# Four output blocks begun together, the first norm moved under the next products, and longer distances between the steps of the head work

## The chip, the cores and the metric

The kernel runs on one core of a Trainium2 chip. The metric is the device time of one execution in microseconds (us). Engines are named as in the profile: PE is TensorE (PEld its weight loads), DVE is VectorE, ACT is ScalarE, POOL is GpSimd, SP is SyncE, which issues nearly all the transfers.

## The reference

One layer of a streaming encoder is computed for two groups of rows that share all weights: 256 prompt rows and 64 rows that continue an earlier stream. Model width is 2048, so the activations are 320 columns wide when they are held feature by feature (16 blocks of 128 features).

```python
h = rmsnorm(x, g_pre_mix);  p = h @ w_in                     # 2048 -> 6144 + 16
a = conformer_conv(value, gate)      # GLU, causal depthwise conv of width 31, group norm, silu
q, k, v = silu(short_conv_4(qkv));  q, k = l2norm(q), l2norm(k)
beta = sigmoid(b);  g = -exp(a_log) * softplus(a_raw + dt_bias)
o, state = gated_delta_chunked(q, k, v, g, beta, state)
b = rmsnorm_per_head(o) * silu(z)
x = x + rmsnorm(concat(a, b) @ w_out, g_post_mix)
h = rmsnorm(x, g_pre_ffn)
gate, up = split(causal_dwconv_3(h @ w_up))                  # 2048 -> 2 * 5632
x = x + rmsnorm((silu(gate) * up) @ w_down, g_post_ffn)
```

The chunked delta rule needs, per chunk and head, the inverse of a unit lower triangular matrix. Outputs are the new rows and the new states of the convolutions and of the delta rule. All values are float32.

## The kernel before, in words

**Products.** Every large product is taken in float32 accuracy by splitting both operands into a rounded part and a rest: `hi` (a copy into the matmul format, ACT, line 174) and `lo` (the difference, DVE, line 175). A block of 128 output columns over half of the depth (8 of 16 feature blocks) takes 24 matmuls of 128x320: 8 times hi*hi (line 190) and hi*lo (line 191), then 8 times lo*hi (line 194). This text calls these matmuls "products" and such a set of 24 a half block. A weight half block is one transfer of 512 KB into one of three buffers `w`; its split goes into one of three pairs `whi`, `wlo`.

**The norm of the input.** The split of x uses x times the gain and not the normed x; the factor per row, `rb`, is multiplied in when a finished block is read from PSUM. So products can start before the norm is known, and everything that reads a finished block waits for `rb`. `rb` comes from sums of squares: a matmul with ones (`pst`, line 212), a small DVE operation and a power on POOL (`rr`, lines 215 and 216), a matmul that spreads it over the partitions (`psb`, line 222), and a copy on ACT.

**The opening.** x and the weights of two blocks (the gate and value of the first convolution block, `first`) are loaded in five groups of k-blocks, 2, 2, 4, 4 and 4 of them. For each group ACT makes hh (line 291) and whi, DVE makes hl and wlo. Squares of x are taken by ACT for two quarters (line 302) and by POOL for two (line 304), and added by DVE (lines 319 and 320). Then come 32 matmuls for the gates (`psba`, lines 249 and 250) on weights `wbz` that are loaded after all those of the opening.

**The plan.** A string orders the blocks of the input projection: `c` is a convolution block (gate and value products, then DVE's 30 taps on `cvt`, line 441), `g` the gates, `h` a head (three blocks, q, k and v, read by DVE and POOL into `qb`, short convolution `cq` at line 504), `z` a head's output gate. Then come 15 blocks of the output projection over 12 of the 16 depth blocks (`psm`), its rest (`psm2`), and the feed-forward part.

**Jobs.** What follows a block (the tail of a convolution block, of a head, the inverse and the recurrence of a pair of heads, the gates) is a generator that yields distances, counted in products: `tick` counts each product, and every 20th it advances the jobs that are due. A job's instructions stand behind the product counted last; within that, the tile scheduler orders each engine's instructions by priority. `finish` empties a job at once, whatever its distances: the tail of convolution block i-2 before block i goes on to its own tail, and pair i-2 before head 2i begins. The order on each engine is fixed when the kernel is built.

The steps that matter here: `pt_c` (line 450) transposes a finished convolution block, its statistics go over DVE, POOL and ACT (`un`), and a second set of transposes (line 465, in the profile also under the name pt_c) brings it back, LAG_STAT later. Head tails make the matrix `np` (line 584) from `pk`, `pks` and the decay factors `E`, which POOL multiplies (line 408) from `psd` (line 404) and `rg` (line 401). A pair's inverse writes `np` to DRAM, reads diagonal blocks back (`dn`), solves them on DVE, and brings the result back through DRAM as `wtp`; LAG_BASE later its first matmuls `pz` (line 652) read `wtp`. After the recurrence, LAG_NORM lies ahead of the transposes `pt_o` (line 781).

PSUM has eight banks: two for blocks (`ps_p`), two for transposes (`ps_t`), four for jobs (`ps_g`).

## Time and profile before

| what | before |
|---|---|
| median of 3 runs (lowest, highest) | 1569.41 us (1567.59, 1575.73) |
| profiled execution, its span | 1568.74 us, 1566.9 us |
| PE, DVE, ACT, POOL busy, share of the span | 97%, 64%, 47%, 21% |
| granted clock, mean | 0.985 |
| input projection and head work | from the opening to about 482.6 us |
| feed-forward part | from about 640 us |

A PE that is busy 97% of the span is read with care: the table of stages shows that its idle time lies nearly all in the first 500 us, and that the granted clock is below full there. So the time is read by where PE waits, by what ended each wait, and by the stretches of half clock behind the waits.

### The profile page before, as it was taken

The page shows a single profiled execution, that of the slowest core. Times are in us where ns is not written, and L with a number is a line of the kernel's source. Part 1 is how long each engine was busy: PE and PEld are TensorE (multiplying, and loading weights), DVE is VectorE, ACT ScalarE, POOL GpSimd, SP SyncE. Part 2 cuts the span into 40 slices and gives each one's busy share as a digit, 9 for nine tenths or more (in the row PEclk, how much of TensorE's full clock was granted, in tenths as well). Part 3 has the DMA queues.
Part 4 walks back from the last instruction along what each step waited for, and adds up shares of the span by engine and source line. Part 5 has one row for each costly group of instructions (what it writes and reads, how often), then busy time and mean ns, then how long its engine had stood idle before and what let it go on. Part 6 is the DMA issues. An engine that isn't in the chain of part 4 may idle for free.

```text
span 1566.9 us, 26507 instructions
## 1 busy us (share of the span) xinstructions
PE 1521.0 (97%) x10247; PEld 1496.3 (95%) x10249; DVE 1009.1 (64%) x1824; ACT 732.2 (47%) x1199; POOL 333.0 (21%) x503
## 2 busy tenths in 40 slices
PE   7998999999989999999999999999999999999998
PEld 6988989999989998899999999999999999999997
DVE  6778869786788567866534665644666544666554
ACT  5664454554635465544434444433444433444453
POOL 4352222242221000122200232200222200222101
PEclk9999999999999999999999999999999999999999
DMA  7435335353443573344455545455444455554453
GB/s 236 141 99 146 107 111 155 111 161 96 117 124 106 152 243 115 117 148 148 123 154 168 150 148 156 126 152 172 149 149 148 133 149 172 150 152 148 134 148 113
DMA packets 95767, 224.31 MB, mean 143 GB/s; under 512 B 18328, under 2 KB 37016, under 8 KB 95512
## 3 DMA queue, kind: packets, MB, share of 16 engines
q1 hardware_dynamic: 95640, 222.61, 47.2%
q8 instruction: 81, 1.33, 0.3%
q14 instruction: 46, 0.38, 0.1%
HBM read 215.45 MB, written 7.12 MB: 142 GB/s over the span
## 4 chain that ended last, share of the span: by engine, by line
PE 80%; DVE 9%; POOL 3%; DMA 3%; ACT 2%; issue 2%; SPq 0%; DVEq 0%; ACTq 0%; POOLq 0%
PE psu L190 12%; PE psu L191 12%; PE psu L194 12%; PE psdn L190 7%; PE psdn L191 7%; PE psdn L194 7%; DVE wlo L175 3%; PE psq L194 2%; PE psq L190 2%; PE psq L191 2%; DVE cvt L441 2%; PE psm L194 2%; PE psm L191 2%; PE psm L190 2%; DMA wtp<-wsp 1%
## 5 line engine op out<-in xcount | busy, mean ns | idle before, releaser
L174 ACT CAST whi<-w 128x1024 fp32r<-128x1024 f32 (+3 forms) x441 | 421.6, 957 | 553.0 <-PE psu L191 172.7
L175 DVE TENSOR_TENSOR wlo<-w,whi 128x1024 fp32r<-128x1024 f32 (+3 forms) x441 | 487.4, 1105 | 186.6 <-ACT whi L174 103.5
L190 PE MATMUL psu<-hi,whi 128*128 128x320 f32 x1344 | 398.2, 310 | 2.9 <-DVE fbuf L980 2.9
L191 PE MATMUL psu<-lo,whi 128*128 128x320 f32 x1344 | 397.9, 310 | 0.0
L190 PEld LDWEIGHTS psu<-hi,whi 128*128 128x128 f32 x1344 | 253.2, 188 | 3.4 <-DVE fbuf L980 3.4
L191 PEld LDWEIGHTS psu<-lo,whi 128*128 128x128 f32 x1344 | 253.1, 188 | 0.0
L981 POOL COPY nffn<-fbuf 128x2 f32<-128x2 f32 x88 | 100.5, 1142 | 597.9 <-DVE fbuf L979 597.2
L194 PE MATMUL psu<-hi,wlo 128*128 128x320 f32 x1344 | 224.8, 309 | 0.0
L191 PE MATMUL psdn<-gl,whi 128*128 128x320 f32 x704 | 208.9, 310 | 0.0
L190 PE MATMUL psdn<-gh,whi 128*128 128x320 f32 x704 | 208.7, 310 | 0.0
L194 PEld LDWEIGHTS psu<-hi,wlo 128*128 128x128 f32 x1344 | 203.9, 188 | 0.0
L979 DVE TENSOR_TENSOR fbuf<-psu,rb 128x256 f32<-128x256 f32 x88 | 37.4, 425 | 176.9 <-PE psu L194 174.4
L441 DVE SCALAR_TENSOR_TENSOR cvt<-ub,par,cvt 128x350 f32<-128x350 f32 x240 | 137.5, 589 | 2.6
L190 PEld LDWEIGHTS psdn<-gh,whi 128*128 128x128 f32 x704 | 132.1, 188 | 0.8 <-ACT gh L198 0.8
L191 PEld LDWEIGHTS psdn<-gl,whi 128*128 128x128 f32 x704 | 132.1, 188 | 0.3
L194 PE MATMUL psdn<-gh,wlo 128*128 128x320 f32 x704 | 124.0, 309 | 0.0
L190 PE MATMUL psq<-hh,whi 128*128 128x320 f32 x384 | 120.0, 325 | 0.0
L191 PE MATMUL psq<-hl,whi 128*128 128x320 f32 x384 | 116.9, 317 | 0.0
L194 PEld LDWEIGHTS psdn<-gh,wlo 128*128 128x128 f32 x704 | 108.5, 188 | 0.0
L190 PEld LDWEIGHTS psq<-hh,whi 128*128 128x128 f32 x384 | 74.4, 194 | 1.0 <-issue 0.7
L191 PEld LDWEIGHTS psq<-hl,whi 128*128 128x128 f32 x384 | 74.4, 194 | 0.8 <-issue 0.7
L194 PE MATMUL psq<-hh,wlo 128*128 128x320 f32 x384 | 69.7, 321 | 0.0
(309 smaller groups left out, 2284.2 us busy)
## 6 DMA issues: line engine op xcount, KB each, us to landing
w<-in_w_up SPq DMA_DIRECT2D x176, 512.0 KB, 3.6
w<-in_w_in SPq DMA_DIRECT2D x95, 512.0 KB, 3.8
w<-in_w_down SPq DMA_DIRECT2D x64, 384.0 KB, 3.1
w<-in_w_down SPq DMA_DIRECT2D x64, 320.0 KB, 2.9
w<-in_w_out SPq DMA_DIRECT2D x32, 384.0 KB, 3.1
w<-in_w_out SPq DMA_DIRECT2D x8, 512.0 KB, 5.7
wtp<-wsp SPq DMA_DIRECT2D x4, 640.0 KB, 6.7
x<-in_x SPq DMA_DIRECT2D x1, 2560.0 KB, 9.4
```

The costliest lines, as they stand in the source:

```text
L174: S.copy(hi[:, 0:width], w[:, 0:width])
L175: V.tensor_tensor(lo[:, 0:width], w[:, 0:width], hi[:, 0:width].bitcast(F32), ALU.subtract)
L190: tick(PE.matmul(ps, wh, xh, start=(k0 + j == 0), stop=False))
L191: tick(PE.matmul(ps, wh, xl, start=False, stop=False))
L194: tick(PE.matmul(ps, lo[:, j * P:(j + 1) * P], xh, start=False, stop=(final and k0 + j == nk - 1)))
L441: V.scalar_tensor_tensor(cvt, ub[:, t:t + 350], pv("w_dw", b * 31 + t), cvt, ALU.mult, ALU.add)
L979: V.tensor_tensor(buf[:, 2:258], psu[:, 0:TP], rb2[:, 0:TP], ALU.mult)
L981: G.tensor_copy(nffn[:, b, 0, :], buf[:, 256:258])
```

## The change

The opening loads a repacked copy of the weights, `w_first`, in which four blocks (8, 0, 24 and 16: gate and value of the first convolution block, two of the three blocks of head 0) lie side by side for each k-block. x and these weights come in k-blocks, singly up to the fourth and then in pairs, on SP; the first part of `par` is loaded by ACT. ACT and DVE are given a fixed order by `then`, k-block by k-block. The four blocks accumulate in two `ps_t` and two `ps_g` banks. All squares of x go to ACT, two k-blocks at a time, and DVE sums them into `ssum`. The gate products now use a `ps_p` bank; behind them the third block of head 0 (32) is multiplied, and `rb` is made by a job during these products: `pst` 24 products behind the four blocks, `psb` 36 later, both rounded up to a multiple of 20. `in_block` hands out finished blocks, so that c0 and h0 multiply nothing. The gates start at once. Distances: LAG_BASE 180 to 280, LAG_STAT 80 to 120, LAG_GATE and LAG_HEAD 40 to 60, LAG_NORM 30 to 60, and in the decay factors 12 to 30.

```diff
-LAG_GATE = 40
+LAG_GATE = 60
-LAG_STAT = 80
-LAG_HEAD = 40
+LAG_STAT = 120
+LAG_HEAD = 60
-LAG_BASE = 180
-LAG_NORM = 30
+LAG_BASE = 280
+LAG_NORM = 60
+LAG_DECAY = 30
...
+FIRST = (8, 0, 24, 16)
+FIRST_V = 32
+NFIRST = len(FIRST)
+FW = NFIRST * P
...
+    def in_block(b, name):
+        if b in ready:
+            return ready.pop(b)
+        ps = ps_p.tile([P, 512], F32, tag="p", name=name)
+        block_matmul(ps[:, 0:T], ins["w_in"][b], hx, (8, 8))
+        return ps
...
+            nc.scalar.dma_start(par[:, 0:NGV], ins["par"][:, 0:NGV])
+            for k in range(0, KB, 2):
+                wg.append(wst.tile([P, HALF], F32, tag="w", name="w"))
+                for kk in ((k, k + 1), (k + 1, k + 2)) if k < 4 else ((k, k + 2),):
+                    load_x(*kk)
+                    load_first(*kk)
...
+            def squares(k):
+                x = xt[k // 4][:, k % 4:k % 4 + 2, :]
+                if k == 0:
+                    then(S, S.activation, ssum, x, AF.Square)
+                else:
+                    sq = xp.tile([P, 2, T], F32, tag="sq", bufs=2, name="sq")
+                    then(S, S.activation, sq, x, AF.Square)
+                    then(V, V.tensor_tensor, ssum, ssum, sq, ALU.add)
...
+                then(S, S.activation, hi_t[k], x, AF.Identity, scale=g)
+                then(V, V.scalar_tensor_tensor, lo_t[k], x, g, hi_t[k].bitcast(F32), ALU.mult, ALU.subtract)
+                if k < 4:
+                    split_part(*pre[-1], wg[k // 2], (k % 2) * FW, FW)
+                elif k % 2:
+                    split_part(*pre[-1], wg[k // 2], 0, 2 * FW)
+                if k % 2 and k >= 5:
+                    squares(k - 5)
...
+        for k0 in range(0, KB, 2):
+            hi, lo = pre[k0 // 2]
+            for ks in ((k0,), (k0 + 1,)) if k0 < 4 else ((k0, k0 + 1),):
+                for wt in (hi, lo):
+                    for k in ks:
+                        for i, b in enumerate(FIRST):
...
+        def first_norm():
+            rr, _ = rstd([ssum[:, 0, :], ssum[:, 1, :]])
+            yield 36, 1, 0
+            S.copy(rb, rstd_rows(rr)[0])
+
+        job = start(first_norm(), 24, 1)
         psba = gate_products(wbz)
-        with tc.high_priority(offset=PRI_E), tc.issue_after(after):
-            S.copy(rb, rstd_rows(rstd([sqs[0][:, 0, :], sqs[0][:, 1, :]])[0])[0])
+        ready[FIRST_V] = in_block(FIRST_V, "psq")
+        finish(job)
...
-            yield LAG_WAIT, 1, 0
+            yield LAG_DECAY, 1, 0
...
-            gates_job = start(gates(), 16)
+            gates_job = start(gates(), 0)
+            advance(gates_job)
```

**ACT in the opening.** hh is the rounded part of x, whi that of the weights, sq a set of squares (128x1280 is four k-blocks, 128x640 two). Before:

```order
L291 ACTIVATE hh_92<-xt_126,par 128x320
L291 ACTIVATE hh_93<-xt_126,par 128x320
L174 CAST whi<-w 128x512
L302 ACTIVATE sq_221<-xt_126 128x1280
L291 ACTIVATE hh_94<-xt_127,par 128x320
L291 ACTIVATE hh_95<-xt_127,par 128x320
L291 ACTIVATE hh_96<-xt_127,par 128x320
L291 ACTIVATE hh_97<-xt_127,par 128x320
L174 CAST whi<-w 128x1024
```

With the change, from the fourth k-block on (L305 is the helper that records the order):

```order
L305 ACTIVATE hh_93<-xt_126,par 128x320
L305 CAST whi<-w 128x512
L305 ACTIVATE hh_94<-xt_127,par 128x320
L305 ACTIVATE hh_95<-xt_127,par 128x320
L305 CAST whi<-w 128x1024
L305 ACTIVATE ssum<-xt_126 128x640
L305 ACTIVATE hh_96<-xt_127,par 128x320
L305 ACTIVATE hh_97<-xt_127,par 128x320
L305 CAST whi<-w 128x1024
```

Before, the weights of four k-blocks stand behind four hh and a square of 1280 columns; with the change those of two k-blocks stand behind two hh and a square of 640.

**PE at the first norm.** psq is a block of head 0, pst the sums, psb the spread factors. Before, four products stand between pst and psb:

```order
L191 MATMUL psq<-hl_109,whi 128x320
L212 MATMUL pst<-cst,sq_221 128x1 x6
L190 MATMUL psq<-hh_94,whi 128x320
L191 MATMUL psq<-hl_110,whi 128x320
L190 MATMUL psq<-hh_95,whi 128x320
L191 MATMUL psq<-hl_111,whi 128x320
L222 MATMUL psb<-cst,rr 128x128 x2
```

With the change, forty (four gate products and 36 of psq, most left out here):

```order
L265 MATMUL psba<-hl_119,wbz 128x320
L220 MATMUL pst<-cst,ssum 128x1 x6
L264 MATMUL psba<-hh_104,wbz 128x320
...
L198 MATMUL psq<-hh_103,whi 128x320
L199 MATMUL psq<-hl_119,whi 128x320
L230 MATMUL psb<-cst,rr 128x128 x2
```

**PE at the tail of the first convolution block.** Its first transposes and those that bring it back (`pt_c<-cst,un`) stand 28 products apart before, and 20 with the change, because there both steps are forced when block c2 goes on. These are the last rows ahead of the second set, before:

```order
L190 MATMUL psgate<-hh_92,whi 128x320
L191 MATMUL psgate<-hl_108,whi 128x320
L190 MATMUL psgate<-hh_93,whi 128x320
L191 MATMUL psgate<-hl_109,whi 128x320
L465 MATMUL pt_c_1382<-cst,un 128x128 x3
L190 MATMUL psgate<-hh_94,whi 128x320
```

and with the change, where the tails of heads 0 and 1 (pk, tkq) now stand at the same place:

```order
L198 MATMUL psgate<-hh_105,whi 128x320
L199 MATMUL psgate<-hl_121,whi 128x320
L609 MATMUL pk<-kq 128x256 x2
L499 MATMUL pt_c_1315<-cst,un 128x128 x3
L579 MATMUL tkq<-cst,kq 128x128 x2
L581 MATMUL tkq<-cst,kq 128x128 x2
L202 MATMUL psgate<-hh_98,wlo 128x320
```

Counted in products on PE, the distance from a pair's last `pks` to its first `pz` was 210, 180, 188 and 197 for the four pairs, and is 280 for each now; from `po` of the last recurrence step to `pt_o` it was 40 for three pairs and 120 for the third, and is 60, 40, 60 and 80.

More of the change, by code (lines that the diff above doesn't have):

```diff
@@ L160, in trunk_kernel @@
     pre = []
+    ready = {}
     def load_dma(src):
@@ L244, in hx @@
         return hi_t[k], lo_t[k]
+    def in_block(b, name):
[4 more added lines that the diff above has]
+        return ps
     def gate_products(wz):
-        psba = ps_g.tile([P, 512], F32, tag="g", name="psba")
+        psba = ps_p.tile([P, 512], F32, tag="p", name="psba")
         for k in range(KB):
@@ L287, in trunk_kernel, with then, split_part @@
             keep_warm(psw, NWARM)
+            last = {}
+            def then(eng, fn, *args, **kw):
+                with ExitStack() as e:
+                    if eng in last:
+                        e.enter_context(tc.issue_after(last[eng].ins))
+                    last[eng] = fn(*args, **kw)
+            def split_part(hi, lo, w, o, n):
+                then(S, S.copy, hi[:, o:o + n], w[:, o:o + n])
+                then(V, V.tensor_tensor, lo[:, o:o + n], w[:, o:o + n], hi[:, o:o + n].bitcast(F32), ALU.subtract)
+            ssum = xp.tile([P, 2, T], F32, tag="ssum", name="ssum")
+            def squares(k):
[6 more added lines that the diff above has]
+                    then(V, V.tensor_tensor, ssum, ssum, sq, ALU.add)
             for k in range(KB):
@@ L317, in trunk_kernel @@
-        with tc.high_priority(offset=PRI_W), tc.issue_after(after.ins):
-            for i in range(1, 4):
-                V.tensor_tensor(sqs[0], sqs[0], sqs[i], ALU.add)
-            V.tensor_tensor(sqs[0][:, 0:2, :], sqs[0][:, 0:2, :], sqs[0][:, 2:4, :], ALU.add)
-        after = dense[0]
+                then(S, S.activation, hi_t[k], x, AF.Identity, scale=g)
+                then(V, V.scalar_tensor_tensor, lo_t[k], x, g, hi_t[k].bitcast(F32), ALU.mult, ALU.subtract)
+                if k % 2 == 0:
+                    pre.append((wsp.tile([P, HALF], F32R, tag="whi", name="whi"), wsp.tile([P, HALF], F32R, tag="wlo", name="wlo")))
@@ new lines, in trunk_kernel @@
+                if k < 4:
[4 more added lines that the diff above has]
+                    squares(k - 5)
+            then(S, S.copy, wbz[:, :, 0:16], wba)
+            then(V, V.tensor_tensor, wbz[:, :, 16:32], wba, wbz[:, :, 0:16].bitcast(F32), ALU.subtract)
+            for k in (KB - 4, KB - 2):
+                squares(k)
+        for i, b in enumerate(FIRST):
+            pool = (ps_t, ps_g)[i // 2]
+            ready[b] = pool.tile([P, 512], F32, tag=pool.name[-1], name="ps_first")
@@ new lines, in trunk_kernel @@
+        for k0 in range(0, KB, 2):
[3 more added lines that the diff above has]
+                    for k in ks:
+                        for i, b in enumerate(FIRST):
+                            ps = ready[b][:, 0:T]
+                            o = (k - k0) * FW + i * P
+                            w = wt[:, o:o + P]
+                            xh, xl = hx(k)
+                            tick(PE.matmul(ps, w, xh, start=(k == 0 and wt is hi), stop=(k == KB - 1 and wt is lo)))
+                            if wt is hi:
+                                tick(PE.matmul(ps, w, xl, start=False, stop=False))
@@ L417, in conv_block @@
     def conv_block(b):
-        if b == 0:
-            psg_, psv = first
-        else:
-            psg_ = ps_p.tile([P, 512], F32, tag="p", name="psgate")
-            block_matmul(psg_[:, 0:T], ins["w_in"][8 + b], hx, (8, 8))
+        psg_ = in_block(8 + b, "psgate")
         ub = ubufs[b % 3]
@@ L428, in conv_block @@
             G.tensor_tensor(sg, sg, rb, ALU.mult)
[L429 to L431 removed]
+        psv = in_block(b, "psv")
         with tc.high_priority(offset=PRI_E):
@@ L491, in qkv_block @@
     def qkv_block(b, dst, dsts, i):
-        psq = ps_p.tile([P, 512], F32, tag="p", name="psq")
-        block_matmul(psq[:, 0:T], ins["w_in"][16 + b], hx, (8, 8))
+        psq = in_block(16 + b, "psq")
         qb = qbufs[i % 2]
```

56 lines of the change are left out of this document (9 added, 47 removed).

## The prediction

> **What bounds the kernel now.** I read the page first, then PE's waits, then busy time by stage, then the granted clock behind the long waits.
>
> ```profile
> PE 1521.0 (97%) x10247; PEld 1496.3 (95%) x10249; DVE 1009.1 (64%) x1824; ACT 732.2 (47%) x1199; POOL 333.0 (21%) x503
> 0.00:25.50 25.50, 20.16 (x105) 16.70 (x106) 17.40 (x22) 15.46 (x25) 8.33 (x10) 0.93 0.71 237
> 25.50:44.00 18.50, 14.86 (x79) 14.33 (x78) 8.59 (x12) 7.44 (x10) 9.10 (x17) 0.77 0.71 210
> 44.00:485.00 441.00, 415.17 (x2830) 405.66 (x2830) 347.84 (x731) 228.57 (x485) 134.51 (x192) 0.97 0.42 122
> 640.00:1540.00 900.00, 896.85 (x6093) 894.47 (x6092) 514.34 (x843) 389.34 (x520) 167.81 (x261) 1.00 0.49 148
> ```
>
> The stages (length, then busy PE, PEld, DVE, ACT and POOL, granted clock) show that the 900 us of the feed-forward part have no room: PE is busy for 896.85 of them at full clock. The change touches nothing there. What can be won lies ahead of 485 us: 5.34 + 3.64 + 25.83 = 34.8 us without PE work, and the time lost at a clock below 1. PE's waits name most of it (total, times, longest):
>
> ```profile
> PE pz L652 <- DMA wtp<-wsp: 13.9, 3, 6.4
> PE ps_first L314 <- ACT whi L174: 4.0, 3, 1.9
> PE pt_o L781 <- ACT kd L567: 3.8, 1, 3.8
> PE psd L404 <- DVE rg L401: 3.5, 3, 2.5
> PE pt_c L465 <- ACT un L461: 2.9, 2, 1.8
> PE psba L249 <- DVE wbz L297: 2.2, 1, 2.2
> PE pz L652 <- DVE wtp L662: 1.7, 1, 1.7
> PE psb L222 <- POOL rr L216: 1.4, 1, 1.4
> PE pt_o L781 <- ACT ot L772: 1.0, 1, 1.0
> ```
>
> Behind the long ones the clock is halved. I looked up every stretch for which it was granted at half (PE busy, clock, DMA):
>
> ```profile
> 15.00:18.41 3.41, 3.41 (x15) 0.50 0.68 260
> 28.65:32.06 3.41, 3.41 (x14) 0.50 0.59 147
> 38.89:45.72 6.83, 6.31 (x25) 0.50 0.37 96
> 93.50:96.91 3.41, 3.25 (x7) 0.50 0.00 0
> 148.12:154.95 6.83, 5.99 (x26) 0.50 0.37 112
> 202.73:206.14 3.41, 3.41 (x15) 0.50 0.46 154
> 352.92:359.75 6.83, 5.86 (x25) 0.50 0.19 72
> 445.07:451.90 6.83, 4.14 (x18) 0.50 0.68 223
> ```
>
> Each follows one of the waits above, and three of the long ones follow the three waits for `wtp`. So a wait of 4 us on PE costs up to 7 us.
>
> **The opening, term A.** The rows for its landmarks on PE, and ACT's and POOL's work there:
>
> ```profile
> 6.76 0.41 PE L314 MATMUL ps_first<-hh,whi 128*128 128x320 f32 x1 [0.99 <-ACT whi L174]
> 9.75 1.27 ACT L302 ACTIVATE sq<-xt 128x1280 f32<-128x1280 f32 x1
> 10.92 1.91 ACT L291 ACTIVATE hh<-xt,par 128x320 fp32r<-128x320 f32 x4
> 15.57 1.03 ACT L174 CAST whi<-w 128x1024 fp32r<-128x1024 f32 x1
> 28.39 0.43 PE L249 MATMUL psba<-hh,wbz 128*128 128x320 f32 x1 [2.21 <-DVE wbz L297]
> 35.90 1.39 PE L212 MATMUL pst<-cst,sq 128*128 128x1 f32 x12
> 39.41 1.54 PE psb L222 x6
> 58.37 1.17 PE psq L194 x8
> 61.89 1.17 PE psq L194 x8
> 137.49 0.31 PE L190 MATMUL psz<-hh,whi 128*128 128x320 f32 x1
> ```
>
> The sets of eight at 58.37 and 61.89 lie one half block apart: 3.52 us for 24 products, 0.147 us each. By 61.89 + 1.17 = 63.06 us PE has done two opening blocks, the gate products, three blocks of head 0 and the norm: five blocks and 32 gate products. Dense, these 272 products would take 40.0 us.
>
> With the change, per pair of k-blocks ACT has two hh, a whi and a square of half the old width: 0.95 + 1.0 + 0.65 = 2.6 us (from the rows of four hh, of whi and of sq). DVE has two hl, a wlo and a sum, by its similar rows about 3 us. PE has 24 products, 3.52 us. So PE sets the pace, where before four k-blocks of ACT work came ahead of each group's products. I let the first product start at 6.3 (the warm-up ends no earlier), add 192 products (28.2) and 1.5 for first landings and ACT's queue: 36.0. In that queue an Exp of the gates, with a table load, now stands between the k-blocks; it waits for the small load of a_log, which moved ahead of the last three weight tiles on SP together with the rest of `par`, and whi of the sixth pair of k-blocks is queued behind it. ACT has 0.9 us a pair to spare, so three pairs absorb it. Weights for the gates are still loaded last, but now have 28 us of products as cover; if that fails, 2.2 us as before. Then 80 products (11.7), `pst` and `psb` at full clock (2.4; the rows show 1.39, and 1.54 at half clock): 50.1 us. The wait for `rr`, 1.4 before, has forty products as cover. Term A is 50.1 - 63.1 = **-13.0**. Bounds: -15 (no wait at all), and -4, if the old loss per product stayed (19.4 us for 96 products, from 6.76 to 28.39 less the wait there, is 5.3 over dense, so 10.6 on 192).
>
> **From there to the end of block c2, term B.** Before, from 63.1 to 137.49, the first product of the block behind it: 74.4 us. Of these 384 products are 56.3, waits 5.3 (psd 3.5, un 1.8), the half clock at 93.5 costs 1.7, and 11.1 remain for the small matmuls of heads and gates. But `rb` now comes at about 48.7 (50.1 less twelve products, plus its copy) and not at 41.4, so all that DVE does with it starts 7 us later, while PE's products run ahead:
>
> ```profile
> 41.45:117.76 76.31, 72.83 (x450) 68.08 (x450) 59.97 (x128) 48.57 (x91) 35.94 (x59) 0.95 0.40 118
> L175 DVE TENSOR_TENSOR wlo<-w,whi 128x1024 fp32r<-128x1024 f32 x16 | 20.1, 1254 | 3.3 <-ACT whi L174 3.1
> L441 DVE SCALAR_TENSOR_TENSOR cvt<-ub,par,cvt 128x350 f32<-128x350 f32 x31 | 18.4, 593 | 0.4
> L504 DVE SCALAR_TENSOR_TENSOR cq<-qb,par,cq 128x323 f32<-128x323 f32 x18 | 10.5, 585 | 0.3 <-ACT cq L502 0.3
> ```
>
> Before, DVE worked 60 us of the 76.3 from `rb` to the first `pt_c`, 16.3 idle. In the new order 13 weight splits lie there instead of 16 and six taps of the next block come in: about 56 us of work, less idling since two blocks of head 0 are ready at once. I put the first convolution block at 105, PE at its `pt_c` at 103.5: a wait of 1.5. Then 20 products (2.9) and some 1.3 of small matmuls stand against the 6 us that the way to `un` took before (28 products and 1.8 of waiting), with POOL's E and head 0's factors ahead of it: 2.8. PSUM and the gates' chain get 1.7. Together 6.0 of waits, and 1.7 for one half clock behind the longest: 75.1 against 74.4, **+0.7**. Bounds -5 (no waits) and +15 (DVE idles as before, see the rivals).
>
> On the clock the Trainium skill ("TensorE: Matmul & The Clock Gate", part 1) has a rule: the gate halves it only after an idle window of about 3.4 us. This trace disagrees: waits of 2.21 (the row at 28.39) and 2.5 us (psd's longest) were enough. By the page the 1.7 above would fall away, and the sum would be 1534.
>
> **The waits for the inverse, term C.** The way to `wtp` before, first pair:
>
> ```profile
> 115.04 0.38 DVE at L588 x2
> 142.30 6.52 DMA wtp<-wsp
> 148.96 2.37 PE pz L652 x10
> ```
>
> From the end of `np` and `at` to the landing at 148.82 it is 33.5 us, and about 3.5 more from `pks`. PE had 210 products, 30.8 us, as cover; now it has 280, 41.1 us, so 4 us remain over. For the other late pairs, 188 and 197 products plus waits of at most 6.4 and little other work give ways of 33 and 36. The cover is again 41.1. So 13.9 us of waits go, and three half clocks of 6.83: half of PE's busy time in them is 8.0, of which I take 7. What is late next? The same jobs, 80 to 100 products later; the last ends under the output projection, which has 540 products. **-20.9**, bounds 0 and -22.
>
> **The longer norm, term D.** The first pair's `pt_o` waited 3.8 with 40 products ahead; 60 now, 2.9 us more, so about 1.2 stay (a head's tail still shares ACT): -2.6. Its half clock (3.41 at 202.73) costs half, -1.5. **-4.1**, bounds 0 and -5.5. **Term E:** the second wait of a convolution tail (2.9 less 1.8) and the 1.0 of the last `pt_o` fall away: **-2.0**. The 1.7 for `wtp` from DVE stays.
>
> **What moving costs, term F.** The first pair's steps now fall into the same slots as the tails of heads 2 and 3 and of blocks c1 and c2. Each step has 20 products, 2.9 us, for a trip over ACT or DVE. The trace shows such step waits of 1.0 to 1.8; I take four of 1.5, **+6.0**. For the tail of c7, which ends 16 products ahead of its use where it had 56, **+0.7**: silu, copy and rest are three passes of some 0.5 us, as hh is, and 3 us behind two weight splits. Bounds 0 and +14. Fewer table loads, longer transfers per row and the repacked weights I cost at nothing: ACT and the DMA queues have idle time under the products (shares of 0.42 and 0.71 above); without it, a table load costs 1.3 us:
>
> ```profile
> L505 ACT ACT_TABLE_LOAD x4 | 5.1, 1283 | 0.1
> ```
>
> **The sum** against the profiled execution's own 1568.74 (span 1566.9 and 1.8 around it; the median is 1569.41, so the two agree): -13.0 + 0.7 - 20.9 - 4.1 - 2.0 + 6.7 = -32.6, **1536 us**.
>
> **The rivals.**
> *DVE takes over behind the norm.* If it idles between `rb` and the first `pt_c` as before, the block is ready at 48.7 + 56 + 16.3 = 121 instead of 105, and PE loses some 15 of term A and B: 1551. For it: 60 of 76.3 busy, and 7 us less time. Against: much of the idling was for blocks PE had not finished, which now are.
> *The steps collide.* Six slots lose up to the 3.8 of `pt_o`, with two half clocks of 6.83 behind them: 16 more than in F, 1552.
> *The distance does not cover.* Weight transfers queue in front of the inverse's on SP, and the way grows from 37 to over 45 us: term C is lost, 1557.
> *Slower.* The opening's eight weight tiles go through three buffers, and x stands between them on SP's queue. If landing, split and release of a tile took 9 us a pair of k-blocks instead of 3.52, term A would be 8 x 5.5 = 44 worse: 1580. It decides from 7.6 us a pair. Against it: the feed-forward part lives on three buffers at 3.52 us a half block.
>
> **How the numbers follow.** Forecast 0.60, DVE 0.17, collisions 0.10, cover 0.08, slower 0.05. The likeliest gives 1536; its own bounds, most terms half way, are 1522 and 1547, and the range goes to 1556 to hold the first two rivals, leaving out the last, part of the cover's and a tail below 1521. 0.5%, 7.8 us, is about what can be told from no change. Faster: all but the slower case and 0.02 of the middle rivals, 0.93; same 0.03; slower 0.04.
>
> **What would show it.** Right: 192 opening products at 3.5 us per 24, ending near 36; `rb` near 49; c2's blocks ending near 125; no `pz` wait for `wtp`; no granted 0.50 near 150, 350 and 440; the feed-forward part starting 33 us earlier. Wrong: waits of `ps_first` for whi or hl, of `pt_c` for `cvt` beyond 5 us, or many 1 to 3 us waits of `px`, `pvn` and `po` between 140 and 220 us.

## The result, and the profile after

| | before | changed |
|---|---|---|
| median (lowest, highest), 4 runs each | 1568.50 us (1565.00, 1575.73) | 1543.84 us (1541.59, 1544.90) |
| ratio to before, 95% interval | | 0.9843 [0.9819, 0.9866] |
| profiled execution, its span | 1568.74 us, 1566.9 us | 1543.88 us, 1542.1 us |
| granted clock, mean | 0.985 | 0.992 |

The change makes the kernel 1.6% faster: 24.7 us where 32.6 were forecast. The page's first row and the stages after (length, then busy PE, PEld, DVE, ACT and POOL, granted clock):

```profile
PE 1513.1 (98%) x10249; PEld 1489.1 (97%) x10249; DVE 1006.5 (65%) x1828; ACT 728.3 (47%) x1203; POOL 332.5 (22%) x501
0.00:25.50 25.50, 24.16 (x146) 21.28 (x146) 17.54 (x27) 21.21 (x35) 2.50 (x7) 1.00 0.90 323
25.50:44.00 18.50, 18.50 (x131) 18.50 (x130) 8.97 (x13) 7.26 (x9) 3.87 (x17) 1.00 0.77 234
44.00:485.00 441.00, 423.45 (x2903) 413.56 (x2902) 369.37 (x773) 231.09 (x499) 145.51 (x192) 0.98 0.42 125
640.00:1540.00 900.00, 896.64 (x6079) 891.10 (x6078) 507.39 (x828) 382.01 (x511) 166.06 (x252) 1.00 0.47 147
```

The opening has become dense: PE is busy for 42.66 of its first 44 us, at full clock, where it was 35.02 of them at a clock of 0.77 to 0.93. The feed-forward part takes as long as before: PE is busy for 896.64 of its 900 us, before for 896.85. From 44 to 485 us PE still does nothing for 17.55 us (25.83 before). What it waits for (total, times, longest), the four groups that matter here:

```profile
PE pt_o L814 <- ACT ot L805: 7.3, 2, 4.2
PE pt_c L484 <- DVE cvt L475: 4.7, 2, 4.2
PE pz L685 <- DVE wtp L695: 2.1, 1, 2.1
PE psg L423 <- DVE gt L412: 0.7, 1, 0.7
```

No `pz` waits for the transfer of `wtp` any more (13.9 us before), and no product of the opening waits for a split. In their place stand the transposes behind the norm, `pt_o`, and those of the first convolution block, `pt_c`. The stretches at half clock lie at the end of these waits or behind them (busy time of PE, PEld, DVE, ACT and POOL, then clock):

```profile
84.05:87.46 3.41, 3.41 (x10) 2.34 (x9) 2.47 (x4) 0.60 (x1) 1.97 (x3) 0.50 0.44 127
107.94:111.35 3.41, 2.97 (x13) 2.98 (x14) 2.79 (x13) 0.32 (x2) 2.57 (x6) 0.50 0.21 84
268.36:275.19 6.83, 6.83 (x29) 6.83 (x30) 6.07 (x12) 1.83 (x4) 0.19 (x1) 0.50 0.35 86
319.56:322.97 3.41, 2.71 (x12) 2.71 (x13) 1.67 (x5) 2.50 (x6) 0.00 (x0) 0.50 0.46 153
415.14:418.55 3.41, 3.08 (x13) 3.08 (x14) 2.16 (x3) 2.16 (x3) 0.86 (x1) 0.50 0.00 0
```

The landmarks on PE, in order of time: the first gate product, the sums of the norm, the first product behind the five opening blocks, the first product behind block c2:

```profile
34.15 0.31 PE L264 MATMUL psba<-hh,wbz 128*128 128x320 f32 x1
38.27 1.40 PE L220 MATMUL pst<-cst,ssum 128*128 128x1 f32 x12
48.83 0.38 PE L198 MATMUL psq<-hh,whi 128*128 128x320 f32 x1 [0.76 <-DVE baT L379]
125.14 0.31 PE L198 MATMUL psz<-hh,whi 128*128 128x320 f32 x1
```

The third row answers to 63.06 us before, where the five blocks were done: 14.2 us are won there. At the fourth (137.49 before) it is 12.35 us, and over the whole execution 24.9. So the first 125 us went as forecast, and the shortfall of 7.8 us lies behind. The feed-forward part's first product (`psu`) starts at 584.1 us. In the profile of before it starts at 608.8, and not at about 640 as the table of before says; so it comes 24.6 us earlier, where the forecast had 33.

**One more view, used for all runs below.** The same products stand at other times and in another order in each kernel, so stretches of time can't be compared directly. I therefore counted PE's work: each PE instruction weighs what usually lies between its start and the next one's (for each kind the median over the profiles, the least for kinds with 20 or fewer). The table gives the time at which a certain amount of work was done, less that amount: what PE had lost by then to waits and slow clock together, in us. A number that stays the same from row to row means dense products.

| work done | before | changed | opening alone (e1) | distances alone (e2) | 180 (e3) | 240 (e9) | old opening, 240 and 100 (e10) |
|---|---|---|---|---|---|---|---|
| 40 us | 18.1 | 3.3 | 3.2 | 11.4 | 3.4 | 3.4 | 17.0 |
| 80 us | 24.1 | 6.7 | 6.0 | 12.9 | 6.7 | 7.1 | 17.2 |
| 120 us | 30.5 | 13.8 | 17.4 | 22.4 | 13.9 | 14.6 | 26.4 |
| 240 us | 40.3 | 15.6 | 33.3 | 24.5 | 26.6 | 17.3 | 28.9 |
| 280 us | 40.6 | 21.2 | 33.5 | 25.7 | 28.4 | 17.9 | 29.5 |
| 320 us | 47.6 | 27.0 | 40.9 | 30.0 | 35.4 | 23.5 | 35.2 |
| 400 us | 56.4 | 32.6 | 51.7 | 34.2 | 42.3 | 23.7 | 35.2 |
| 600 us | 67.6 | 42.8 | 63.1 | 45.8 | 54.9 | 35.4 | 48.3 |

The changed kernel's remaining losses have places: 7 us between 80 and 120, and 17 between 240 and 400. That is where the experiments look. The 10 to 13 us between 400 and 600, the last tails and the step to the feed-forward part, stand in every column.

### The profile page after: what moved, and what is told of

It is laid out like the page before. It is cut to its first block, busy times and chain, and to the rows that moved or that the text cites. A ratio compares the mean times of both kernels' runs of the same rounds, so it can differ in the third digit from the quotient of the medians.

```text
span 1542.1 us, 26538 instructions
## 1 busy us (share of the span) xinstructions
PE 1513.1 (98%) x10249; PEld 1489.1 (97%) x10249; DVE 1006.5 (65%) x1828; ACT 728.3 (47%) x1203; POOL 332.5 (22%) x501
## 4 chain that ended last, share of the span: by engine, by line
PE 80%; DVE 12%; POOL 3%; ACT 2%; issue 2%; DMA 1%; SPq 0%; DVEq 0%; ACTq 0%; POOLq 0%
PE psu L202 13%; PE psu L198 13%; PE psu L199 13%; PE psdn L198 7%; PE psdn L199 7%; PE psdn L202 7%; DVE wlo L183 4%; DVE cvt L475 3%; PE psq L202 2%; PE psq L198 2%; PE psq L199 2%; PE psm L202 1%; PE psm L198 1%; PE psm L199 1%; PE ps_first L352 1%
## 5 line engine op out<-in xcount | busy, mean ns | idle before, releaser
L182 ACT CAST whi<-w 128x1024 fp32r<-128x1024 f32 (+2 forms) x432 | 411.3, 954 | 516.7 <-PE psu L199 170.7
L183 DVE TENSOR_TENSOR wlo<-w,whi 128x1024 fp32r<-128x1024 f32 (+2 forms) x432 | 477.1, 1105 | 198.1 <-ACT whi L182 111.4
L198 PE MATMUL psq<-hh,whi 128*128 128x320 f32 x352 | 106.1, 315 | 0.8 <-DVE baT L379 0.8
L199 PE MATMUL psq<-hl,whi 128*128 128x320 f32 x352 | 104.9, 311 | 0.0
L198 PEld LDWEIGHTS psq<-hh,whi 128*128 128x128 f32 x352 | 66.9, 190 | 1.1 <-ACT whi L182 1.0
L199 PEld LDWEIGHTS psq<-hl,whi 128*128 128x128 f32 x352 | 66.9, 190 | 0.0
L1057 DVE TENSOR_TENSOR y<-y,psdn 128x320 f32<-128x320 f32 x48 | 23.4, 488 | 63.9 <-PE psdn L202 63.9
```

Of the source, the lines that this page charges most:

```text
L182: S.copy(hi[:, 0:width], w[:, 0:width])
L183: V.tensor_tensor(lo[:, 0:width], w[:, 0:width], hi[:, 0:width].bitcast(F32), ALU.subtract)
L198: tick(PE.matmul(ps, wh, xh, start=(k0 + j == 0), stop=False))
L199: tick(PE.matmul(ps, wh, xl, start=False, stop=False))
L1057: V.tensor_tensor(y[:, n, :], y[:, n, :], psd[:, 0:T], ALU.add)
```

## Experiments

The theory: the forecast's terms A to C hold, and the shortfall is term F, the work that was moved and now meets other work at `pt_o` and `pz` of later pairs. The rivals: the waits come from distances that are too short or from forced places, and not from a collision; or VectorE sets the pace behind the opening whatever the distances are.

| run | what differs | median, us | ratio to before |
|---|---|---|---|
| e1 | before's distances, new opening | 1565.18 | 0.9982 [0.9968, 0.9996] |
| e2 | before's opening, new distances | 1549.35 | 0.9878 [0.9857, 0.9899] |
| e3 | changed, behind the inverse 180 | 1559.76 | 0.9958 [0.9942, 0.9974] |
| e4 | changed, norm 30 | 1549.02 | 0.9874 [0.9856, 0.9892] |
| e5 | changed, norm 100 | 1545.20 | 0.9843 [0.9807, 0.9878] |
| e6 | changed, behind the inverse 240, norm 100 | 1537.24 | 0.9799 [0.9772, 0.9825] |
| e7 | changed, other order of blocks | 1553.69 | 0.9903 [0.9876, 0.9930] |
| e8 | e6 and e7 together | 1549.69 | 0.9881 [0.9848, 0.9914] |
| e9 | changed, behind the inverse 240 | 1535.99 | 0.9808 [0.9792, 0.9824] |
| e10 | before's opening, else as e6 | 1548.59 | 0.9888 [0.9861, 0.9916] |
| e11 | e6, decay steps in another order | 1534.29 | 0.9798 [0.9782, 0.9813] |
| e12 | changed, first norm begun at once | 1542.97 | 0.9855 [0.9839, 0.9871] |

e1 to e4 ran on one chip, e5 to e8 on one, e9 to e12 on one, each group with its own runs of the kernel before (medians 1567.96, 1569.41 and 1565.93 us). Within a group times are compared, between groups ratios. The changed kernel ran in none of these groups, so a time beside its 1543.84 us is a rough comparison, and its ratio of 0.9843 [0.9819, 0.9866] is the safer one.

### The two halves of the change: e1 and e2

```diff
 e1, on the changed kernel          e2, on the kernel before
-LAG_GATE = 60                     -LAG_GATE = 40
+LAG_GATE = 40                     +LAG_GATE = 60
-LAG_STAT = 120                    -LAG_STAT = 80
+LAG_STAT = 80                     +LAG_STAT = 120
-LAG_HEAD = 60                     -LAG_HEAD = 40
+LAG_HEAD = 40                     +LAG_HEAD = 60
-LAG_BASE = 280                    -LAG_BASE = 180
+LAG_BASE = 180                    +LAG_BASE = 280
-LAG_NORM = 60                     -LAG_NORM = 30
+LAG_NORM = 30                     +LAG_NORM = 60
-LAG_DECAY = 30                    -            yield LAG_WAIT, 1, 0
+LAG_DECAY = 12                    +            yield 30, 1, 0
```

> The changed kernel with the six old distances (gates 40, statistics 80, heads 40, inverse 180, norms 30, decay 12 products): the four blocks begun together, the ScalarE squares and the first norm as a job stay. In the changed kernel the block behind the first norm began 14.1 us earlier than before, and only 12.4 us more were won between 125 us and the feed-forward. If the two parts simply add, this one keeps the first gain and loses the second: some 14 us under the kernel before, ratio 0.991 (1554 of 1568), with the wait for wtp (10 us and more over the four pairs) back at the z products. Rival: the old distances also hurt the opening (gates after 40 products and the statistics after 80 no longer hide the norm's tail), and it gains under 9 us, with waits over 2 us at psg or pt_c before 125 us.

> The kernel before with only the six new distances; the opening is the old one. If the parts add, the gain is the 12.4 us that the changed kernel wins behind 125 us: ratio 0.992 (1556 of 1568), no wait for wtp, and waits of 4.2 and 3.0 us or so at pt_o of pairs 1 and 2 as in the changed kernel, since what makes them (the next pair's inverse on VectorE ahead of the outputs, the forced place of po) doesn't depend on the opening. Rival, that these waits come from the opening's shift of all later work: pt_o waits under 2 us in all, and a gain of 16 us or more (ratio 0.990 or less).

The opening alone gains 2.8 us, the distances alone 18.6, both 24.7. For e1 the rival holds in its number: nearly all of the head start is lost again. It doesn't hold in its place, since `psg` waits 1.4 us and `pt_c` less; the long wait ahead of 125 us is another one, at `tv`. PE's waits in e1:

```profile
PE pz L685 <- DMA wtp<-wsp: 14.5, 3, 6.9
PE tv L583 <- ACT vT L538: 6.1, 1, 6.1
PE pt_o L814 <- ACT kd L600: 3.6, 1, 3.6
```

And the timeline of POOL and ACT in e1, ahead of the second of these waits:

```profile
92.82 4.79 POOL L448 TENSOR_TENSOR E<-eg,cst 128x64 f32<-128x64 f32 x8 [0.71 <-ACT eg L445]
97.64 0.60 ACT L445 ACTIVATE eg<-psd 128x512 f32<-128x512 f32 x1 [3.97 <-POOL E L448]
101.95 0.42 ACT L538 ACTIVATE vT<-cq 128x256 f32<-128x256 f32 x1
```

`rg` and `eg` take two buffers in turn, so `eg` always gets the same one, and each exponential on ACT waits until POOL has multiplied the one before into `E`. With distances of 40 for the head and 12 for the decay steps, head 0's `vT` stands behind two of these on ACT, and the transposes of `vT` wait 6.1 us on PE. In the table e1 loses 11.4 us between 80 and 120, before 6.4. Then the waits for `wtp` come at the old places.

e2's gain is larger than the 12.4 us that were expected; its `pt_o` waits are 5.6 us and more, as the theory had them. PE's waits in e2:

```profile
PE pt_c L465 <- ACT un L461: 7.1, 1, 7.1
PE pt_o L781 <- ACT ot L772: 5.6, 2, 3.1
```

Part of the surplus is not the distances' doing. PE's instructions stand in the same order in both old openings up to about 45 us, yet e2 had lost 11.4 us by the row of 40 and the profiled execution of before 18.1. e10, again with this opening, had lost 17.0. So the old opening's length varies by some 7 us from one execution to another (it has stretches at half clock around 38 to 45 us in some and not in others), while in all eleven profiles with the new opening that number lies between 3.0 and 4.4.

### The distance behind the inverse and the norm's distance: e3 and e4

```diff
 e3                   e4
-LAG_BASE = 280      -LAG_NORM = 60
+LAG_BASE = 180      +LAG_NORM = 30
```

> The changed kernel with the distance behind the inverse back at 180 products. Theory (term C of the sum): the waits for wtp come back at the z products, about 14 us of wait and half-clock stretches with them; but the recurrence's products then stand earlier against the next pair's inverse, so that the 7.3 us of waits at pt_o shrink to 2 or less. Net +8 to +16 us on the changed kernel, ratio to the kernel before 0.990 to 0.994. Rival, that pt_o waits because 60 products are too short for the norm wherever it stands: pt_o keeps its 7 us and the time is 18 us or more over the changed kernel, near the kernel before less its opening (ratio 0.995 or over).

> The changed kernel with the distance of the norm's products back at 30. Theory (term D): 30 products are about 6.4 us at the spacing of the products, 60 are 12.8; the wait at pt_o in pair 2 grows from 3.0 by up to 6 us, pairs 0 and 3 get waits of up to 4 us, pair 1 (whose place is forced) stays or grows by 2; in sum +8 to +14 us with the half clock behind them, ratio to the kernel before 0.989 to 0.994. Rival, that the distance hardly matters because the chain behind po is late for another reason (the products that come between are themselves held up): less than 4 us over the changed kernel.

The distance behind the inverse is worth the most of all single numbers: e3 lies 15.9 us over the changed kernel's 1543.84 (some 18 by the ratios). Its waits at `pz` are back, and those at `pt_o` fall from 7.9 us to 3.0. PE's waits in e3:

```profile
PE pz L685 <- DMA wtp<-wsp: 5.6, 1, 5.6
PE pz L685 <- POOL nqkv L533: 4.5, 1, 4.5
PE pz L685 <- POOL nqkv L532: 3.2, 1, 3.2
PE pt_o L814 <- ACT kd L600: 2.2, 2, 1.4
```

The three long waits are at the places of e1's waits for `wtp`. In two of them a copy on POOL is named, which ended at 155.1 us in the first case. But `pz` reads only `wtp` and `nm`, and POOL had made `nm` by 123.9. The transfer of `wtp` was issued at 149.65; in the changed kernel it takes 5.2 us to land, which would put this landing at 154.9 and `pz` right behind it, at 155.23. So the transfer is the likelier cause; its landing isn't in this trace. That `pt_o` waits less with the recurrence further ahead is what the theory said. But the order changed as well: 82, 80, 100 and 60 products lie between `po` and `pt_o` here, where the changed kernel has 60, 40, 60 and 80, so the two causes aren't separated.

e4 lies 5.2 us over, between the theory's 8 and the rival's 4: 12.1 us of waits at `pt_o` against 7.3, in four places. All four `pt_o` now follow `po` by 40 products, since jobs are only advanced every 20th product. Pair 2 thus loses 20 products, 2.9 us at 0.147 us each, and its wait grows by 3.0, from 3.01 to 6.04. So the distance counts in full there. (The 6.4 us that the expectation gives for 30 products are too many: at 0.147 us each they are 4.4.) PE's longest group of waits in e4:

```profile
PE pt_o L814 <- ACT ot L805: 12.1, 4, 6.0
```

### Longer norm, shorter distance behind the inverse: e5, e6 and e9

```diff
 e5                  e6                   e9
-LAG_NORM = 60      -LAG_BASE = 280      -LAG_BASE = 280
+LAG_NORM = 100     +LAG_BASE = 240      +LAG_BASE = 240
                    -LAG_NORM = 60
                    +LAG_NORM = 100
```

> The changed kernel with the norm's distance at 100. In pair 2 the products at pt_o then follow po by 100 products instead of 60; in pair 1 the forced finish ahead of block pair h6 keeps them at 40. Theory (the distance alone decides): pair 2's 3.0 us at pt_o go, with their half-clock stretch (0.7 us), pair 1's 4.2 us stay: 3 to 5 us under the changed kernel, near 1540, ratio to the kernel before 0.981 to 0.983. Rival (VectorE behind: its output step comes late behind the next pair's inverse, whatever the distance): pair 2 still waits over 1.5 us at pt_o, or the wait moves to the statistics of c5 and c6 (pt_c), and the time is within 2 us of the changed kernel.

> The changed kernel with the distance behind the inverse at 240 and the norm's at 100: pair 1's recurrence ends before it is forced, and its pt_o follows po by 76 products instead of 40. Theory (distance): both waits at pt_o (7.3 us) go and two half-clock stretches with them (1.6 us at least, up to 3.5); 240 products are still enough for wtp in all pairs, or cost up to 3 us in the one whose DMA is slowest. In sum 4 to 10 us under the changed kernel, 1534 to 1540, ratio 0.978 to 0.982. Rival (wtp's DMA needs more than 240): waits for wtp of 3 us or more come back in one pair or more and eat the gain: 1541 to 1548.

> The changed kernel with 240 products behind the inverse and the norm's distance left at 60. It tells which of the two numbers won the 6.6 us of the run with 240 and 100 (1537.2). Its pt_o follow po by 60, 76, 60 and 60 products. Theory (pair 1's forced place was the loss, and 100 behind po alone had won nothing): within 3 us of 1537. Rival (the norm's distance matters once pair 1 is free): pair 2's wait at pt_o stays at about 3 us with its half-clock stretch, and 3 to 5 us are missing: 1540 to 1543.

e5 gives nothing (1545.20): the wait of pair 2 goes and comes back at the statistics of a convolution block, so the rival was right. PE's waits in e5:

```profile
PE pt_c L484 <- DVE cvt L475: 9.8, 2, 5.1
PE pt_o L814 <- ACT ot L805: 4.3, 1, 4.3
```

e6 takes 1537.24 us, within its theory's range. e9, with 240 alone, has the whole gain: 1535.99, a ratio of 0.9808, against 0.9799 for e6; the two can't be told apart. How large the gain over the changed kernel is, the medians and the ratios tell differently: 7.9 and 5.5 us, and the two intervals touch. In the profiles, `psu` starts 7.7 us earlier in e9. The rival that the norm's distance matters is out.

But the theory's place was wrong too. In the changed kernel pair 1's `pt_o` is forced, 40 products behind `po`; in e9 76 products lie between, and its first half waits for nothing. Yet a wait of 4.0 us stands there still, in e6 as well: the second half needs the bank in which a convolution tail's `pt_c` lies, until `un` has read that. PE's waits in e9:

```profile
PE pt_c L484 <- DVE cvt L475: 5.9, 2, 4.6
PE pt_o L814 <- ACT un L495: 4.0, 1, 4.0
PE pz L685 <- DVE wtp L695: 1.9, 2, 1.2
```

The table shows where the gain lies: between 240 and 280 (5.6 us lost by the changed kernel, 0.6 by e9) and between 320 and 400 (5.6 against 0.2). Between 280 and 320, where pair 1's `pt_o` stands, both lose nearly the same (5.8 and 5.6).

The first place is pair 1's `pz`, which waits 2.1 us, with 6.83 us of half clock behind it. It waits for an addition to `wtp` on DVE; six taps of a convolution block, from 263.13 to 266.80, stand ahead of that. e2 has the same 280 products and the old opening, and loses only 1.2 us there, while e4, e5 and e12, with 280 and the new opening, wait 2.1 to 3.4 us at this place. So the distance alone doesn't make this wait; it takes the earlier opening too.

The second place is pair 2's `pt_o`. The timeline of DVE, POOL, ACT and PE in the changed kernel:

```profile
404.27 1.21 DVE L183 TENSOR_TENSOR wlo<-w,whi 128x1024 fp32r<-128x1024 f32 x1
406.02 0.20 DVE L647 TENSOR_TENSOR tmp<-wi,dn 40x50 f32<-40x50 f32 x1
406.14 0.41 DVE L790 TENSOR_TENSOR ot<-qs,po 128x256 f32<-128x256 f32 x1
410.11 1.93 POOL L803 TENSOR_TENSOR t<-t,sc 128x5 f32<-128x5 f32 x1
412.07 1.28 ACT L805 ACTIVATE ot<-ot,t 128x128 f32<-128x128 f32 x4 [3.79 <-POOL t L803]
413.36 1.28 ACT L463 ACT_TABLE_LOAD   x1
414.66 0.47 ACT L463 ACTIVATE sg<-sg 128x320 f32<-128x320 f32 x1
415.03 0.39 ACT L805 ACTIVATE ot<-ot,t 128x128 f32<-128x128 f32 x1
415.48 1.54 PE L814 MATMUL pt_o<-cst,ot 128*128 128x128 f32 x6 [3.01 <-ACT ot L805]
```

L790 is the pair's last output step, L647 a step of the next pair's inverse, L463 the sigmoid of a convolution block. In both kernels 60 products lie between `po` and `pt_o`, and PE needs the same 10.0 us for that way (402.47 to 412.46 here, 392.21 to 402.23 in e9). What differs is the chain from the first `po` to the last scaled `ot`: 12.95 us here, 9.11 in e9. Of these 3.84 us, some 0.6 lie ahead of L790, which starts 3.67 us behind `po` here and 3.10 in e9. There the weight split and the inverse's steps stand in DVE's queue. Another 1.5 lie in POOL's four small steps, which take from 407.41 to 412.04 here and from 396.58 to 399.70 in e9; no run shows why. The largest part, 1.8, lies on ACT, where a table load and the sigmoid stand between the fourth and the fifth block of `ot`. So the moved recurrence does meet other work, but on three engines, and what can be put down to the next pair's inverse is the smallest part. e2, with 280 as well, has the same order on ACT and a wait of 3.07 us. In e9 the recurrence stands 40 products earlier, and nothing stands between the five blocks of `ot` on ACT. The instructions on `ot` from 380 to 420 us in e9 (count, shortest/median/longest in ns, first and last start):

```profile
L814 PE MATMUL pt_o<-cst,ot x6: 271/272/273, 402.2 to 402.8; 128*128 128x128 f32 x6
L805 ACT ACTIVATE ot<-ot,t x5: 388/388/402, 399.7 to 400.9; 128x128 f32<-128x128 f32 x5
L790 DVE TENSOR_TENSOR ot<-qs,po x1: 411/411/411, 395.3 to 395.3; 128x256 f32<-128x256 f32 x1
```

So 280 was too long and 180 too short: at 180 PE waits for the inverse, at 280 pair 1's `pz` and the end of pair 2 run into other work, and at 240 these waits are 1.2 us and nothing. Only pair 1's `pt_o` waits about as long as before.

### Another order of blocks: e7 and e8

```diff
-PLAN = "c0 g h0 h1 c1 z0 c2 z1 h2 h3 z2 z3 c3 h4 h5 c4 z4 h6 h7 c5 z5 c6 z6 z7 c7"
+PLAN = "c0 g h0 h1 c1 z0 z1 c2 h2 h3 z2 z3 c3 h4 h5 c4 z4 z5 h6 h7 c5 c6 z6 z7 c7"
```

e8 has 240 and 100 besides.

> The changed kernel with another order of blocks (z1 ahead of c2, z5 ahead of h6): c0's transposes at pt_c then stand at product 608 instead of 580, 4.1 us later, and pair 1's forced end comes 48 products later but still with only 44 products between po and pt_o. Theory: the 4.2 us at pt_c and the half-clock stretch behind it (0.6 us) go, pair 1's and pair 2's pt_o waits stay within 2 us of 4.2 and 3.0: 3 to 6 us under the changed kernel, 1538 to 1541. Rival (VectorE is behind by then and c2's own work waits instead): the wait moves to the next conv or head job and the time is within 2 us of the changed kernel.

> The two edits together: the other order of blocks, 240 products behind the inverse, 100 behind po. All four pt_o then follow po by 100 products and none is forced. Theory: no wait over 1 us at pt_o or pt_c between 100 and 480 us; the changed kernel loses 13.9 us of it up to 120 us' worth of products and 20 us between there and the feed-forward, about 12 of them at these places: 8 to 13 us under the changed kernel, 1531 to 1536, ratio 0.976 to 0.979. Rival (the work of VectorE, over 90 of 110 us busy in the stretch from 330 to 440, is what is late): 1537 or more, with waits of 2 us and more at other places of that stretch.

Both lose. c0's wait goes, but others take its place (in both, `pks` waits 2.7 us and two waits for `un` total over 6), and the last convolution blocks now lie closer together; that their tails find too few products there is likely, but not shown. In e8 that end costs some 11 us between 420 and 440 us of work, counted as in the table. Between 120 and 400, where all four `pt_o` stand 100 products behind `po`, e8 loses only some 8 us, the changed kernel 18.8. So this doesn't speak against the distances; the order of blocks was a bad way to get room. PE's waits in e8:

```profile
PE pt_c L499 <- ACT un L495: 6.4, 2, 4.4
PE pks L613 <- ACT vh L605: 2.7, 1, 2.7
```

### What the opening is worth: e10

```diff
-LAG_BASE = 180
+LAG_BASE = 240
-LAG_NORM = 30
+LAG_NORM = 100
```

(on the kernel before, with the other new distances as in e2)

> The kernel before with its own opening and all the new distances, but 240 behind the inverse and 100 behind po. It tells what the four-block opening is worth where pair 1 is not forced: with 280 and 60 it was worth 5.5 us (1549.35 against 1543.84), though its block behind the norm began 14.1 us earlier than in the profiled run of before and 8.2 us earlier than in the profile of the old opening with new distances. Theory (the rest of the head start was lost at pair 1's forced place): it is now worth 8 to 11 us, so this kernel takes 1545 to 1549. Rival (VectorE sets the pace behind the opening whatever the distances): worth 6 us or less again, 1541 to 1543.

e10 takes 1548.59 in the group in which e9 takes 1535.99 and e11 1534.29. That is 12.6 us over e9, from which it differs in the opening and in the norm's distance; against e6, which differs in the opening alone, the ratios are 0.9888 and 0.9799, some 14 us. So with 240 the whole head start reaches the end, a little more than the 8 to 11 us of the theory; with 280 and 60 the opening was worth 5.5, with the old distances 2.8. If VectorE set the pace behind the opening whatever the distances, it couldn't be worth 13 here. The step from 5.5 to 13 is in part the old opening's own length, which was longer in e10's profile than in e2's. What the profiles show without that: with 280 the new opening is 8.1 us ahead by the row of 40 (e2 against changed) and 3.0 by the row of 600; with 240 it is 13.6 ahead (e10 against e9) and still 12.9 at the end.

### The wait at 104 us: e11

```diff
-for c, h0, w in ((0, 0, 4), (1, 0, 4), (2, 0, 8), (0, 4, 4), (1, 4, 4)):
+for c, h0, w in ((0, 0, 4), (1, 0, 4), (0, 4, 4), (1, 4, 4), (2, 0, 8)):
```

> The kernel with 240 and 100, with the decay step of the short last chunk (eight GpSimd products of 64 columns, 4.84 us together) moved from third to last of the five. In the changed kernel ScalarE's next exponential waits 4.0 us for it, two weight splits stand behind that on ScalarE, the rest of the split behind them on VectorE (idle 2.3 us), and c0's transposes wait 4.2 to 4.6 us for the convolution. Theory: that chain is the cause, so the wait at pt_c near 103 us falls to 2.5 us or less, and the half-clock stretch behind it shortens: 2 to 4 us under 1537. Rival (the convolution is late by VectorE's own work): the wait stays over 3.5 us and the time within 1.5 us of 1537.

The chain in the changed kernel, from POOL over ACT and DVE to PE:

```profile
93.09 4.84 POOL L448 TENSOR_TENSOR E<-eg,cst 128x64 f32<-128x64 f32 x8 [0.71 <-ACT eg L445]
97.97 0.60 ACT L445 ACTIVATE eg<-psd 128x512 f32<-128x512 f32 x1 [4.02 <-POOL E L448]
98.46 1.98 ACT L182 CAST whi<-w 128x1024 fp32r<-128x1024 f32 x2
99.53 1.49 DVE L183 TENSOR_TENSOR wlo<-w,whi 128x1024 fp32r<-128x1024 f32 x1 [2.06 <-ACT whi L182]
108.38 0.90 PE L484 MATMUL pt_c<-cst,cvt 128*128 128x128 f32 x3 [4.17 <-DVE cvt L475]
```

A row of small multiplications on POOL holds up ACT, ACT holds up a weight split, the split holds up DVE's convolution taps, and PE waits for these. e11 moves the eight short products to the end of the line, and PE's wait, 4.62 us in e6, falls to 2.63, nearly the 2.5 of the theory. So 2.0 us of the wait are this chain; what the rest waits for isn't shown. The row of e11's timeline:

```profile
106.86 0.55 PE L484 MATMUL pt_c<-cst,cvt 128*128 128x128 f32 x3 [2.63 <-DVE cvt L475]
```

The time is 1.7 us under e9's in the same group, from which it also differs in the norm's distance, and the ratio 0.9798 next to e6's 0.9799 can't be told from it; the wait shows the cause, the time by itself doesn't. Its median is the lowest of the study, and its interval lies wholly under that of the changed kernel.

### The norm as a job: e12

```diff
         job = start(first_norm(), 24, 1)
+        finish(job)
         psba = gate_products(wbz)
         ready[FIRST_V] = in_block(FIRST_V, "psq")
-        finish(job)
```

> The changed kernel with the first norm not a job: its sums and its broadcast are begun straight behind the opening's 192 products instead of behind 24 gate products, and finished before the next block is begun in program order. In the changed kernel the sums start at 38.3 us and the broadcast at 45.5, with all products between them dense. Theory (the job hides the norm's chain): the broadcast now follows about 20 gate products, 2.9 us, and waits some 4 us for the reciprocal root on GpSimd, with half-clock behind it: 3 to 7 us over the changed kernel, 1547 to 1551. Rival (the sums' chain starts 4 us earlier and the tail of the gates with it, which gives later what is lost here): within 2 us of the changed kernel.

No difference: 1542.97 us. The rival's number holds, though nothing is lost in the place that it meant. PE doesn't wait for the reciprocal root; the order of the instructions still puts twenty gate products between the sums and the broadcast. POOL's power and the broadcast's weight loads in e12's timeline:

```profile
36.72 0.86 POOL L224 TENSOR_TENSOR rr<-rr,nhalf 128x3 f32<-128x3 f32 x1 [7.12 <-DVE rr L223]
39.11 0.78 PEld L230 LDWEIGHTS psb<-cst,rr 128*128 128x128 f32 x6
```

The sums end at 36.38 us and `rr` is ready at 37.58, so the 2.9 us of the twenty products cover it. `rb` then comes some 6 us earlier, and c0's wait for `cvt` is down to 0.5 us, but head 0's `kd` and the first `un` are waited for instead, 3.6 and 2.7 us. So what the opening brings doesn't come from the later norm; the four dense blocks remain.

## Why the prediction was right, and where it was off

The forecast was 1536 us with a range of 1521 to 1556; the kernel takes 1543.84.

The sum adds its terms as if each stood alone. The runs say otherwise: the opening alone brings 2.8 us, and beside the new distances 5.5 (e2 against the changed kernel), though it is 12.35 us ahead at 125 us. What it brings to the end hangs on the distances behind it, which the forecast didn't say.

**Term A** (-13.0, and five blocks done at 50.1): right. The first product started at 5.81, where the forecast had 6.3 because of the warm-up matmuls, which had ended by 5.77 in before's trace too. The opening's products ended at 34.2 instead of 36.0, and the next block began at 48.83, 14.2 us earlier than before. That this fits so well is in part luck: it is counted from before's profiled opening, one of the long ones; e2's old opening lost 6.7 us less.

**Term B** (+0.7): right as a sum (+1.9), wrong in its parts, whose errors cancel by luck. `pt_c` was forecast to wait 1.5 us and the second transposes 2.8; they waited 4.2 and 0.4. The forecast named POOL's E among what stands ahead of `un`, and missed that E also stands, over ACT's queue and a weight split, ahead of the convolution itself; e11 shows that chain for 2.0 us of the wait.

**Term C** (-20.9): right. The 13.9 us of waits and the three long half-clock stretches behind them are gone, and with 180 (e3) waits as long come back in three places, 15.9 us of time. Its question, what is late next, was answered with "the same jobs, 80 to 100 products later". That was the omission: the jobs that come later stand among other work on DVE, POOL and ACT, and are late there.

**Term D and E** (-4.1, -2.0): the first pair's `pt_o` lost its wait as forecast, and the last one's fell from 1.0 to 0.6 us. But the term stopped at these; pairs 1 and 2, counted from 0, had no wait there before and now have 4.25 and 3.01 us.

**Term F** (+6.7) is the step that was mis-sized, and it was looked for in the wrong place. It took four waits of 1.5 us in the first pair, where waits of 1 to 3 us between 140 and 220 us would have shown it. Nothing of the kind is there. What the trace shows in its place is 7.3 us at `pt_o` of pairs 1 and 2 (pair 1's at a forced place), 2.1 at pair 1's `pz`, and three half-clock stretches of 13.65 us in all behind them, for which F had nothing and which cost about half their length. Behind c2 the forecast summed to -20.3 and the profile gives -12.5; with the other terms as they were, F measured about 14.5, just over its upper bound of 14. e9 takes pair 2's wait away and shortens the one at `pz` to 1.2 us, by one number: by the row of 600 it has lost 35.4 us, the changed kernel 42.8.

**The rivals.** DVE took over in one place only, by 4.2 us at `pt_c` and not 15. *The steps collide* was the right mechanism at half its price (7.8 us over F where it had 16), in other pairs than F had named; what collides is traced above for pair 2 alone. The distance covered, and the opening's three buffers held.

## What to carry to other kernels

A longer distance between a producer and its consumer takes away one wait and moves all that follows; so look for what the moved work meets next, in the later rounds of the loop and not only in the first, and try distances on both sides of the one that just covers (here 180, 240, 280). An opening that ends earlier is worth what the stretch behind it lets through: the same opening was worth 3, 5 and 13 us (between the last two, the old opening's own length also varied), so the two belong together in one measurement. When a wait's releaser is busy, follow its queue back engine by engine; here a 4.84 us row of GpSimd stood, over two other engines, behind a wait of TensorE of 4.2 to 4.6 us, and moving the row took 2.0 us of it away.

## What the runs showed of the hardware

**The clock.** Stretches at half clock last multiples of 3.41 us and can follow waits that are shorter than that. Nearly all waits of 2 us and more ahead of 500 us were followed by one or overlapped with one; it began within the wait or up to 1.7 us behind it, or was running already (in e7). In the changed kernel 2.11 us at 266.1 were enough for 6.83 us from 268.36. But the same wait of 2.11 us, at 268.4 in e12, was followed by none, nor were two in e2, of 2.0 and 3.07 us; behind one of 2.70 at 104.6 in e12 half clock came only with the next wait. Shorter ones went both ways: in e9 one of 1.32 us at 433.4 was followed by half clock from 434.77, one of 1.23 at 256.1 wasn't, nor was one of 1.49 at 450.9 in e4. Even the 0.66 us before `psg`, with the small matmuls behind it, was followed by half clock from 84.05 in the changed kernel, but not in e4 and e6 with the same wait. So one wait has no one price. The length of 3.41 us is that of the window which the Trainium skill ("TensorE: Matmul & The Clock Gate", part 1) gives, and the page lets it run freely, by which the same wait could fall well or badly; its condition of a whole idle window isn't what these rows show.

**GpSimd's short products.** The decay factors on POOL in the changed kernel, from the groups by shape between 80 and 110 us: eight products of 128x64 took 4.8 us, sixteen of 128x128 10.6. The mean of one is 638 and 689 ns, so half the columns cost nearly the same. The means vary: in e11 they are 620 and 777 ns.

```profile
L448 POOL TENSOR_TENSOR E<-eg,cst 128x128 f32<-128x128 f32 x16 | 10.6, 689 | 3.6 <-ACT eg L445 3.6
L448 POOL TENSOR_TENSOR E<-eg,cst 128x64 f32<-128x64 f32 x8 | 4.8, 638 | 0.7 <-ACT eg L445 0.7
```
